# A transformer trunk on one core: the neighbourhood stage's keys and queries split once and arranged by DMA copies, its small softmax blocks scaled by a product with a broadcast

## The chip, the cores and the metric

One core of a Trainium2 chip. The metric is the device time of one execution in microseconds (us). The kernel before was executed three times: 2248.18, 2249.1 and 2251.29 us, median 2249.1 us.

## What is computed

Four residual steps in each of two layers, on 512 tokens of width 1024, all in float32: a half-step SwiGLU network, a token mixer, cross-attention into 256 memory tokens and a second half-step network, each followed by a layer norm. The mixer of the second layer is the one that the change touches, 2-D neighbourhood attention with 16 heads of width 64:

```python
def mixer_c(h, w_in, w_out, rpb):
    ...
    q, k, v = jnp.split(h @ w_in, 3, axis=-1)
    ...
    def row_block(r):
        rs = jnp.clip(r - kh // 2, 0, rows - kh)
        ...
        s = jnp.einsum('bwhd,bawjhd->bhwaj', q_r, k_nb).astype(jnp.float32) * scale
        s = s + bias.astype(jnp.float32)[None]
        p = jax.nn.softmax(s.reshape(B, C_HEADS, GRID_W, kh * kw), axis=-1)
        ...
        return jnp.einsum('bhwaj,bawjhd->bwhd', p, v_nb)
    ...
    return o @ w_out
```

## The kernel before

**Numbers.** A float32 operand is kept as two parts, high (rounded to the type that TensorE reads) and low (what is left), and each product is three matmuls (`mm3`, high x high, high x low, low x high). Making the two parts out of a PSUM bank takes a ScalarE instruction, which copies the high part, and a VectorE instruction, which subtracts it from the bank (`split`, line 293). Weights are loaded by SyncE (SP) into a `raw` tile of up to 1 MB and split in the same way (`weights`, line 310).

**Order.** No engine's order is written by hand. `Graph` records every operation (`record`, lines 128 to 163; every instruction is issued from the one call in it, so that the profile shows L140 throughout), and derives from overlapping tiles what must come before what. `emit` (lines 165 to 247) then plays the engines forward with a price for each operation (`cost`, line 110; a DMA of SP is priced at its bytes by 205 GB/s, at least 600 ns, and 2000 ns more until others may use it) and with the free buffers of each tag (`BUFS`: 14 of `t2`, 27 of `slab`, 2 of `raw`, and PSUM banks `a` 3, `d` 2, `t` 3), and issues the instructions engine by engine in the order that comes out. The semaphores are put in afterwards by the framework. All DMAs of SP share one hardware queue, and SP waits, in order, for what each of its DMAs needs.

**Stages.** ffn, mixer AB, memory, ffn, ffn, mixer C (`mixer_c`, line 914), memory, ffn. Mixer C goes by eight pairs of heads. For each pair `keys` (line 952) projects 128 columns into a `t` bank with 24 matmuls, and `queries` (line 937) into a `d` bank (the first pair's into `a` banks). The bank's rows 0 to 63 belong to the pair's first head, 64 to 127 to the second. The scores contract over 128 rows, of which a head fills 64; the other 64 hold further parts of the same head, so that two matmuls do for three: the queries' tile of a head has its high part on its own 64 rows and its low part on the other 64, and the keys have for each head one tile with the high part on both halves and one with the low part on both. Before, ScalarE and VectorE write these halves directly from the bank: per head one 64x512 instruction of each for the queries, and two of each for the keys.

`weights_of` (line 987) makes the scores of a head's four query blocks (`a` banks), adds the bias tables (`biases`, line 967, loaded by a DMA of POOL), and the softmax; blocks 0 and 3 (128x192) are scaled on VectorE, 1 and 2 (128x256) on POOL (`normalise`, line 618). `turned` (line 1017) transposes them into `t` banks and splits those; `attend` (line 1030) multiplies with the values into `d` banks. The main loop (line 1057) records, for a pair: keys of the next, `turned`, queries of the one after, `weights_of` the next, `attend`, and two blocks of `values`. The memory stages scale one 128x256 block in two on VectorE, in eight pairs per stage; `weights_a` in mixer AB scales blocks of 512 columns.

Of the kernel before, what the change touches and what calls it, by code (L numbers as in the profile page):

```python
# [12 lines left out]
F32 = mybir.dt.float32  # L13
# [3 lines left out]
AF = mybir.ActivationFunctionType  # L17
ALU = mybir.AluOpType
# [45 lines left out]
class Graph:  # L64
# [63 lines left out]
    def record(self, engine, method, args, kw):  # L128
        kw = dict(kw)
        aps = [z for z in list(args) + list(kw.values()) if hasattr(z, "tensor")]  # L130
        outs = [kw[k] for k in ("out", "accum_out") if k in kw]
        if "out" not in kw:
            outs.insert(0, args[0])
        ins = [z for z in aps if not any(z is o for o in outs)]
        op = Op()
        op.engine, op.index, op.dma = engine, len(self.ops), method == "dma_start"
        op.rank = op.index
        op.ns = self.cost(engine, method, outs[0], ins, kw)
        fn = getattr(getattr(self.nc, engine), method)
        op.call = lambda: fn(*args, **kw)  # L140
        op.deps, op.users, op.frees = set(), [], []
        if self.after and engine in self.after[1]:
            op.deps.add(self.after[0])
        for z, writes in [(z, False) for z in ins] + [(z, True) for z in outs]:
            info = self.tiles.get(z.tensor.name)
            if info is None:
                continue
            p0, p1, runs = self.extent(z)
            opens = writes and kw.get("start", False)
            keep = []  # L150
            for q, w, a0, a1, other in info["log"]:
                over = opens or p0 < a1 and a0 < p1 and (
                    info["bank"] and q.engine != engine or any(l < b and a < h for l, h in runs for a, b in other)
                )
                if over and (w or writes) and q is not op:
                    op.deps.add(q)
                covered = writes and p0 <= a0 and a1 <= p1 and all(any(l <= a and b <= h for l, h in runs) for a, b in other)
                if not covered:
                    keep.append((q, w, a0, a1, other))
            keep.append((op, writes, p0, p1, runs))  # L160
            info["log"] = keep
            info["users"].add(op)
        self.ops.append(op)
# [86 lines left out]
class Kernel:  # L250
# [365 lines left out]
        return h, l  # L616

    def normalise(self, u, r, on_vector):
        if on_vector:
            self.nc.vector.tensor_scalar(u, u, r, None, ALU.mult)  # L620
        else:
            self.nc.gpsimd.tensor_tensor(out=u, in0=u, in1=r.broadcast_to(list(u.shape)), op=ALU.mult)

    def softmax(self, u, rows, mn, lo, n, sums=None, on_vector=False):

# [288 lines left out]
    def mixer_c(self, ln_i, last):  # L914
        nc, a = self.nc, self.a
# [21 lines left out]
        def queries(pair, first=False):  # L937

            if pair % 2 == 0:
                wq[0] = self.w_cols(w_in, 128 * pair)  # L940
            ps = self.ps("a" if first else "d")
            for lo, hi in [(0, 128), (128, 256), (256, 512)] if first else [(0, 512)]:
                self.project(wq[0][pair % 2], ps, lo, hi)
            qs[pair] = self.pair()
            for s, z in enumerate(qs[pair]):
                own, other = slice(64 * s, 64 * s + 64), slice(64 - 64 * s, 128 - 64 * s)
                nc.scalar.activation(z[own], ps[own], AF.Copy, scale=-0.125)
                nc.vector.scalar_tensor_tensor(
                    out=z[other], in0=ps[own], scalar=-0.125, in1=z[own].bitcast(F32), op0=ALU.mult, op1=ALU.subtract
                )  # L950

        def keys(pair, first=False):

            if pair % 2 == 0:
                wk[0] = self.w_cols(w_in, D + 128 * pair)
            ps = self.ps("a" if first else "t")
            for lo, hi in [(0, 256), (256, 512)] if first else [(0, 512)]:
                self.project(wk[0][pair % 2], ps, lo, hi)
            ks[pair] = [self.pair() for _ in range(2)]
            for s, (h, l) in enumerate(ks[pair]):  # L960
                own, other = slice(64 * s, 64 * s + 64), slice(64 - 64 * s, 128 - 64 * s)
                for half in (own, other):
                    nc.scalar.copy(h[half], ps[own])
                for half in (own, other):
                    nc.vector.tensor_tensor(out=l[half], in0=ps[own], in1=h[own].bitcast(F32), op=ALU.subtract)

        def biases(pair):

# [88 lines left out]
        vp, qs, ks, acts = {}, {}, {}, []  # L1057
        wv, wq, wk, wo = [None], [None], [None], {}
        for t in range(NT):
            values(0, t)  # L1060
        queries(0, True)
        keys(0, True)
        queries(1)
        us = weights_of(0)
        for pair in range(8):


            if pair < 7:
                keys(pair + 1)
            else:  # L1070
                for n in range(3, 5):
                    share(n)
            pts = turned(us)
            if pair < 6:
                queries(pair + 2)
            else:
                for n in (0, 1) if pair == 6 else (5, 6, 7):
                    share(n)
            if pair < 7:
                us = weights_of(pair + 1)  # L1080
            acts.append(attend(pts, pair))
            if pair < 6:
                for t in range(2):
                    values(pair // 2 + 1, 2 * (pair % 2) + t)
            elif pair == 6:
                share(2)
# [200 lines left out]
```

## Time and profile before

| | |
|---|---|
| runs | 2248.18, 2249.1, 2251.29 us (median 2249.1) |
| profiled execution: its time | 2250.06 us |
| profiled execution: its span, first to last instruction | 2248.3 us |
| mean granted TensorE clock | 0.996 |
| stretch of mixer C | about 1495 to 1670 us |
| stretch of mixer AB | about 394 to 560 us |

PE is TensorE's matmuls, PEld its weight loads beside them, DVE is VectorE, ACT ScalarE, POOL GpSimd, SP SyncE. The span and the profiled execution's time differ by 1.8 us, which lie before the first and after the last instruction. `slab`, `t2` and `raw` are tiles in SBUF; `a`, `d` and `t` as an output of PE are PSUM banks, and since the views leave buffer numbers out, the `t2` tiles also appear there as `t`.

### The profile page before, as it was taken

How to read it: one execution, taken by the hardware profiler on the slowest of the kernel's cores; microseconds unless marked ns; L12 is line 12 of the kernel's file. 1: busy time of each engine (PE TensorE's matmuls, PEld its weight loads, DVE VectorE, ACT ScalarE, POOL GpSimd, SP SyncE). 2: the span in 40 equal slices, each digit the busy share in tenths (PEclk: the TensorE clock that was granted, in tenths of full speed). 3: DMA queues.
4: the chain of work that ended last, by engine and by line, in shares of the span. 5: the costliest groups of instructions: out<-in, count | busy, mean ns of one | idle time of the engine just before them, and what ended most of it. 6: DMA issues, size and time to landing. Idle time of an engine off the chain costs nothing. (4 is left out here: it accounts for less than half of the span.)

```text
span 2248.3 us, 28157 instructions
## 1 busy us (share of the span) xinstructions
PE 2207.0 (98%) x11312; PEld 1871.7 (83%) x11312; DVE 1420.1 (63%) x2116; ACT 882.7 (39%) x1418; POOL 287.0 (13%) x391
## 2 busy tenths in 40 slices
PE   8999999999999999999999999999999999999998
PEld 7888888778898888888888888888888988888886
DVE  5666646788745766665655667368776457666653
ACT  4323332566433433333333333256554434333331
POOL 0000203543000100001100003013411001000011
PEclk9999999999999999999999999999999999999999
DMA  6333241003333332225312334212233333322241
GB/s 207 129 120 113 67 154 57 20 20 90 124 106 113 113 113 90 72 83 168 105 40 86 113 117 150 75 62 68 69 113 96 129 113 113 113 82 72 85 137 38
DMA packets 168755, 221.09 MB, mean 98 GB/s; under 512 B 6192, under 2 KB 136880, under 8 KB 168624
## 3 DMA queue, kind: packets, MB, share of 16 engines
q1 hardware_dynamic: 165552, 208.80, 28.9%
q0 software_dynamic: 3072, 10.49, 1.3%
q8 instruction: 89, 1.46, 0.3%
q14 instruction: 42, 0.34, 0.1%
HBM read 217.17 MB, written 4.19 MB: 98 GB/s over the span
## 5 line engine op out<-in xcount | busy, mean ns | idle before, releaser
L140 PE MATMUL a<-xh,slab 128*128 128x512 f32 (+1 forms) x2960 | 890.8, 382 | 0.0
L140 PEld LDWEIGHTS a<-xh,slab 128*128 128x128 f32 x2960 | 549.1, 188 | 107.1
L140 PE MATMUL d<-slab,slab 128*128 128x512 f32 (+2 forms) x2432 | 572.5, 384 | 4.7 <-DVE slab L140 2.8
L140 PE MATMUL a<-xl,slab 128*128 128x512 f32 (+1 forms) x1480 | 565.0, 382 | 0.0
L140 PEld LDWEIGHTS d<-slab,slab 128*128 128x128 f32 x2432 | 441.1, 188 | 94.3 <-DVE slab L140 4.2
L140 ACT CAST slab<-raw 128x1024 fp32r<-128x1024 f32 x316 | 320.7, 1050 | 310.9 <-DMA raw<-ffn_w_gate 129.8
L140 DVE TENSOR_TENSOR slab<-raw,slab 128x1024 fp32r<-128x1024 f32 x316 | 391.6, 1254 | 72.9 <-ACT slab L140 55.4
L140 PEld LDWEIGHTS a<-xl,slab 128*128 128x128 f32 x1480 | 278.3, 188 | 53.0
L140 DVE TENSOR_TENSOR slab<-slab,slab 128x1024 fp32r<-128x1024 f32 (+2 forms) x208 | 241.4, 1184 | 18.9 <-ACT slab L140 17.6
L140 ACT CAST slab<-slab 128x1024 fp32r<-128x1024 f32 (+1 forms) x144 | 140.1, 1000 | 238.4 <-DVE slab L140 238.3
L140 ACT CAST slab<-t 128x512 fp32r<-128x512 f32 (+3 forms) x261 | 143.5, 572 | 225.9 <-DVE t L140 142.0
L140 PE MATMUL a<-slab,slab 128*128 128x256 f32 (+3 forms) x1336 | 204.9, 303 | 6.2 <-DVE slab L140 2.6
L140 DVE TENSOR_TENSOR slab<-a,t 128x512 f32<-128x512 f32 x56 | 38.7, 691 | 269.3 <-PE a L140 269.3
L140 PEld LDWEIGHTS a<-slab,slab 128*128 128x128 f32 x1336 | 180.6, 194 | 21.5 <-DVE slab L140 6.0
L140 DVE TENSOR_TENSOR slab<-t,slab 128x512 fp32r<-128x512 f32 (+3 forms) x261 | 164.3, 654 | 42.7 <-ACT slab L140 41.5
L140 DVE SCALAR_TENSOR_TENSOR x<-d,x 128x512 f32<-128x512 f32 x216 | 147.3, 685 | 48.3 <-PE d L140 47.3
L140 PE MATMUL t<-slab,slab 128*128 128x512 f32 (+1 forms) x648 | 152.1, 379 | 0.0
L140 ACT ACTIVATE t<-a 128x512 f32<-128x512 f32 (+2 forms) x104 | 57.4, 552 | 225.2 <-PE a L140 203.0
L140 POOL TENSOR_TENSOR x<-x,slab 128x512 f32<-128x512 f32 x24 | 46.0, 1950 | 780.7 <-DVE x L140 780.7
L140 PEld LDWEIGHTS t<-slab,slab 128*128 128x128 f32 x648 | 115.7, 188 | 25.0 <-DVE slab L140 2.2
L140 POOL TENSOR_TENSOR t<-t,l 128x256 f32<-128x256 f32 (+2 forms) x104 | 80.1, 785 | 308.4 <-DVE l L140 308.4
L140 PE MATMUL a<-slab,xh 128*128 128x256 f32 (+1 forms) x432 | 98.1, 319 | 4.1 <-ACT xh L140 4.0
(97 smaller groups left out, 1810.0 us busy)
## 6 DMA issues: line engine op xcount, KB each, us to landing
raw<-ffn_w_gate SPq DMA_DIRECT2D x40, 1024.0 KB
raw<-ffn_w_up SPq DMA_DIRECT2D x40, 1024.0 KB
slab<-ffn_w_down SPq DMA_DIRECT2D x64, 512.0 KB
raw<-ffn_w_down SPq DMA_DIRECT2D x12, 1024.0 KB
raw<-mem_w_kv SPq DMA_DIRECT2D x8, 1024.0 KB
raw<-mem_w_kv SPq DMA_DIRECT2D x16, 512.0 KB
raw<-mem_w_q SPq DMA_DIRECT2D x8, 1024.0 KB
raw<-mem_w_o SPq DMA_DIRECT2D x8, 1024.0 KB
```

Of the source, the lines that this page charges most:

```text
L140: op.call = lambda: fn(*args, **kw)
```

## The change

Three edits. In `record`, two reads of one PSUM bank by different engines become an ordering dependency of the planner. In `normalise`, blocks of up to 256 columns on VectorE are scaled with `tensor_tensor` and a broadcast of the reciprocal in place of `tensor_scalar`: 32 blocks of 128x192 in mixer C and 16 of 128x256 in the memory stages. In mixer C, each bank of keys or queries is split once, with all 128 rows, into two `t2` tiles, and SP copies halves of 64x512 (128 KB) from there into the same `slab` tiles as before: 4 copies per pair for the queries, 8 for the keys, 96 in all.

```diff
--- before.py
+++ after.py
@@ -152,7 +152,7 @@
                 over = opens or p0 < a1 and a0 < p1 and (
                     info["bank"] and q.engine != engine or any(l < b and a < h for l, h in runs for a, b in other)
                 )
-                if over and (w or writes) and q is not op:
+                if over and (w or writes or info["bank"] and q.engine != engine) and q is not op:
                     op.deps.add(q)
                 covered = writes and p0 <= a0 and a1 <= p1 and all(any(l <= a and b <= h for l, h in runs) for a, b in other)
                 if not covered:
@@ -616,10 +616,10 @@
         return h, l
 
     def normalise(self, u, r, on_vector):
-        if on_vector:
-            self.nc.vector.tensor_scalar(u, u, r, None, ALU.mult)
-        else:
-            self.nc.gpsimd.tensor_tensor(out=u, in0=u, in1=r.broadcast_to(list(u.shape)), op=ALU.mult)
+        if on_vector and u.shape[1] > 256:
+            return self.nc.vector.tensor_scalar(u, u, r, None, ALU.mult)
+        engine = self.nc.vector if on_vector else self.nc.gpsimd
+        engine.tensor_tensor(out=u, in0=u, in1=r.broadcast_to(list(u.shape)), op=ALU.mult)
 
     def softmax(self, u, rows, mn, lo, n, sums=None, on_vector=False):
 
@@ -941,13 +941,14 @@
             ps = self.ps("a" if first else "d")
             for lo, hi in [(0, 128), (128, 256), (256, 512)] if first else [(0, 512)]:
                 self.project(wq[0][pair % 2], ps, lo, hi)
+            parts = self.t2(), self.t2()
+            self.split(ps, *parts, scale=-0.125)
             qs[pair] = self.pair()
             for s, z in enumerate(qs[pair]):
-                own, other = slice(64 * s, 64 * s + 64), slice(64 - 64 * s, 128 - 64 * s)
-                nc.scalar.activation(z[own], ps[own], AF.Copy, scale=-0.125)
-                nc.vector.scalar_tensor_tensor(
-                    out=z[other], in0=ps[own], scalar=-0.125, in1=z[own].bitcast(F32), op0=ALU.mult, op1=ALU.subtract
-                )
+                for i, part in enumerate(parts):
+                    nc.sync.dma_start(
+                        out=z[64 * i : 64 * i + 64].bitcast(F32), in_=part[64 * s : 64 * s + 64].bitcast(F32)
+                    )
 
         def keys(pair, first=False):
 
@@ -956,13 +957,15 @@
             ps = self.ps("a" if first else "t")
             for lo, hi in [(0, 256), (256, 512)] if first else [(0, 512)]:
                 self.project(wk[0][pair % 2], ps, lo, hi)
+            parts = self.t2(), self.t2()
+            self.split(ps, *parts)
             ks[pair] = [self.pair() for _ in range(2)]
-            for s, (h, l) in enumerate(ks[pair]):
-                own, other = slice(64 * s, 64 * s + 64), slice(64 - 64 * s, 128 - 64 * s)
-                for half in (own, other):
-                    nc.scalar.copy(h[half], ps[own])
-                for half in (own, other):
-                    nc.vector.tensor_tensor(out=l[half], in0=ps[own], in1=h[own].bitcast(F32), op=ALU.subtract)
+            for s, both in enumerate(ks[pair]):
+                for z, part in zip(both, parts):
+                    for i in range(2):
+                        nc.sync.dma_start(
+                        out=z[64 * i : 64 * i + 64].bitcast(F32), in_=part[64 * s : 64 * s + 64].bitcast(F32)
+                    )
 
         def biases(pair):
```

The order on the engines around the keys of the fourth pair (pair 3), first **SP**. Before, only weight loads stand there (`raw_2340` is the keys' weights of pairs 4 and 5, `raw_2401` the queries' of 6 and 7, `raw_2331` and `raw_2438` are for values):

```order
L140 DMA raw_2294_2375<-c_w_in 128x8x256
L140 DMA raw_2331_2412<-c_w_in 128x4x256 x2
L140 DMA raw_2340_2421<-c_w_in 128x8x256
L140 DMA raw_2401_2482<-c_w_in 128x8x256
L140 DMA raw_2438_2519<-c_w_in 128x4x256 x2
L140 DMA raw_2447_2528<-c_w_in 128x8x256
```

After (`t2_2298` and `t2_2299` are the high and low part of the keys, `slab_2300` and `slab_2301` hold the keys' two tiles of the first and of the second head; `t2_2316` and `t2_2317` are the queries' parts of pair 4, and the first row is a copy of the queries of pair 3; `raw_2358` and `raw_2425` are the two loads named above):

```order
L140 DMA slab_2264_2345<-t2_2263_2344 64x512 x2
L140 DMA raw_2358_2439<-c_w_in 128x8x256
L140 DMA raw_2425_2506<-c_w_in 128x8x256
L140 DMA slab_2300_2381<-t2_2298_2379 64x512 x2
L140 DMA slab_2300_2381<-t2_2299_2380 64x512 x2
L140 DMA slab_2301_2382<-t2_2298_2379 64x512 x2
L140 DMA slab_2301_2382<-t2_2299_2380 64x512 x2
L140 DMA slab_2318_2399<-t2_2316_2397 64x512
L140 DMA slab_2318_2399<-t2_2317_2398 64x512
L140 DMA slab_2318_2399<-t2_2316_2397 64x512
```

Eight copies of the keys now stand in SP's queue, four for each head, and right ahead of them two weight loads of 1 MB; behind them are the four copies of the queries.

**ACT**, the same place. Before (`t_2283` is the keys' bank; the 128x512 casts split the transposes of the pair before):

```order
L140 CAST slab_2284_2365<-t_2283_2364 64x512 x2
L140 CAST slab_2285_2366<-t_2283_2364 64x512
L140 CAST slab_2287_2368<-t_2286_2367 128x512
L140 CAST slab_2289_2370<-t_2288_2369 128x512
L140 CAST slab_2285_2366<-t_2283_2364 64x512
L140 CAST slab_2291_2372<-t_2290_2371 128x512
L140 CAST slab_2293_2374<-t_2292_2373 128x512
L140 CAST slab_2341_2422<-raw_2340_2421 128x1024
L140 ACTIVATE slab_2300_2381<-d_2299_2380 64x512 x2
```

After (`t_2297` is the keys' bank):

```order
L140 CAST t2_2298_2379<-t_2297_2378 128x512
L140 CAST slab_2303_2384<-t_2302_2383 128x512
L140 CAST slab_2305_2386<-t_2304_2385 128x512
L140 CAST slab_2307_2388<-t_2306_2387 128x512
L140 CAST slab_2309_2390<-t_2308_2389 128x512
L140 CAST slab_2359_2440<-raw_2358_2439 128x1024
L140 ACTIVATE t2_2316_2397<-d_2315_2396 128x512
```

Four casts of 64 rows, with the splits of two transposed banks between them, have become one of 128 rows, ahead of all four transposed banks. The same holds on VectorE.

**PE**, after the keys of pair 3 and the first head's two transposes: `d_2299` is the bank of the queries of pair 4, the `ident` rows are the second head's transposes. Before, the last of the 14 matmuls into `d_2299` that stand ahead of those transposes, and what follows:

```order
L140 MATMUL d_2299_2380<-xh_2_83,slab_2295_2376 128x512
L140 MATMUL d_2299_2380<-xl_3_84,slab_2295_2376 128x512
L140 MATMUL t_2290_2371<-ident_1_78,t2_2266_2347 128x128 x3
L140 MATMUL t_2290_2371<-ident_1_78,t2_2267_2348 128x128
L140 MATMUL t_2292_2373<-ident_1_78,t2_2267_2348 128x128 x2
L140 MATMUL t_2292_2373<-ident_1_78,t2_2266_2347 128x128
L140 MATMUL t_2292_2373<-ident_1_78,t2_2267_2348 128x128
L140 MATMUL d_2299_2380<-xh_2_83,slab_2296_2377 128x512
```

After (the bank of queries is `d_2315`, and these are all of its matmuls that stand ahead):

```order
L140 MATMUL t_2304_2385<-ident_1_78,t2_2270_2351 128x128
L140 MATMUL d_2315_2396<-xh_2_83,slab_2311_2392 128x512
L140 MATMUL d_2315_2396<-xl_3_84,slab_2311_2392 128x512
L140 MATMUL d_2315_2396<-xh_2_83,slab_2312_2393 128x512
L140 MATMUL d_2315_2396<-xh_2_83,slab_2311_2392 128x512
L140 MATMUL t_2306_2387<-ident_1_78,t2_2280_2361 128x128 x3
L140 MATMUL t_2306_2387<-ident_1_78,t2_2281_2362 128x128
L140 MATMUL d_2315_2396<-xl_3_84,slab_2311_2392 128x512
L140 MATMUL t_2308_2389<-ident_1_78,t2_2281_2362 128x128 x2
L140 MATMUL t_2308_2389<-ident_1_78,t2_2280_2361 128x128
L140 MATMUL t_2308_2389<-ident_1_78,t2_2281_2362 128x128
```

The second head's transposes have moved forward, from behind 14 of the 24 query matmuls to behind 4.

## Rows read from the trace of the kernel before

**Rows 1.** The page's head: span, and busy time, share and instructions of engines.

```profile
span 2248.3 us, 28157 instructions
PE 2207.0 (98%) x11312; PEld 1871.7 (83%) x11312; DVE 1420.1 (63%) x2116; ACT 882.7 (39%) x1418; POOL 287.0 (13%) x391
```

**Rows 2.** Stretches (two ffn, mixer AB, mixer C): length, busy, clock, DMA.

```profile
1100.00:1475.00 375.00, 374.88 (x1793) 314.56 (x1792) 235.21 (x291) 127.34 (x166) 39.98 (x47) 1.00 0.29 96
394.00:560.00 166.00, 162.03 (x877) 134.18 (x876) 135.35 (x350) 103.51 (x248) 76.36 (x120) 1.00 0.16 40
1495.00:1670.00 175.00, 171.20 (x1046) 148.98 (x1045) 136.92 (x306) 112.72 (x257) 59.37 (x106) 1.00 0.23 76
```

**Rows 3.** Waits of PE in mixer C: us in total, times, longest.

```profile
PE t L140 <- DVE slab L140: 1.3, 3, 0.6
PE a L140 <- DVE mn L140: 1.2, 4, 0.6
PE d L140 <- DVE slab L140: 0.9, 4, 0.3
```

**Rows 4.** VectorE's groups in mixer C: count, busy, mean ns, idle before.

```profile
L140 DVE TENSOR_TENSOR slab<-t,slab 128x512 fp32r<-128x512 f32 x35 | 24.6, 734 | 0.4
L140 DVE TENSOR_TENSOR slab<-t,slab 64x512 fp32r<-64x512 f32 x28 | 19.3, 689 | 23.6 <-ACT slab L140 23.3
L140 DVE TENSOR_SCALAR t<-t,l 128x192 f32<-128x192 f32 x32 | 19.0, 632 | 0.3
...
L140 DVE CUSTOM_DVE_ANT_0 t<-a,t 128x192 f32<-128x192 f32 x32 | 10.8, 350 | 2.4 <-PE a L140 2.4
L140 DVE SCALAR_TENSOR_TENSOR slab<-d,slab 64x512 fp32r<-64x512 f32 x14 | 9.6, 689 | 1.3 <-ACT slab L140 1.1
```

**Rows 5.** ScalarE's groups in mixer C.

```profile
L140 ACT CAST slab<-t 128x512 fp32r<-128x512 f32 x35 | 19.8, 595 | 5.7 <-PE t L140 3.1 <-DVE t L140 2.3
L140 ACT CAST slab<-t 64x512 fp32r<-64x512 f32 x28 | 16.2, 580 | 30.8 <-PE t L140 25.3 <-DVE slab L140 5.2
...
L140 ACT ACTIVATE slab<-d 64x512 fp32r<-64x512 f32 x14 | 8.3, 593 | 10.0 <-PE d L140 9.9
```

**Rows 6.** Timeline around the keys of pair 3: start, us, engine, what.

```profile
1557.23 0.39 PE L140 MATMUL t<-xh,slab 128*128 128x512 f32 x1
...
1565.13 0.88 PE L140 MATMUL a<-slab,slab 128*128 128x192 f32 x6
1565.84 0.40 PE L140 MATMUL d<-slab,slab 128*128 128x256 f32 x2
...
1557.72 1.17 ACT L140 CAST slab<-t 64x512 fp32r<-64x512 f32 x2 [2.66 <-PE t L140]
...
1560.25 4.76 DVE L140 TENSOR_TENSOR slab<-t,slab 64x512 fp32r<-64x512 f32 x7 [0.65 <-ACT slab L140]
```

**Rows 7.** Timeline at the first pair: end of its keys, first scores.

```profile
1497.49 0.28 PE L140 MATMUL a<-xh,slab 128*128 128x256 f32 x1
...
1502.85 0.88 PE L140 MATMUL a<-slab,slab 128*128 128x192 f32 x6
```

**Rows 8.** DMAs of POOL (us to landing), and SP's issues (ns min/median/max).

```profile
t<-bias POOLq DMA_DIRECT2D x16, 128.0 KB, 2.4
...
L140 SPq DMA_DIRECT2D raw<-c_w_in x16: 367/368/529, 1404.1 to 1602.0; - x16
...
L140 SPq DMA_DIRECT2D bias<-rpb_g x16: 631/662/1044, 33.0 to 156.7; - x16
```

**Rows 9.** Timeline of one 1 MB load of SP and the cast that waits for it.

```profile
1176.86 0.37 SPq L140 DMA_DIRECT2D raw<-ffn_w_up  x1
...
1182.24 1.05 ACT L140 CAST slab<-raw 128x1024 fp32r<-128x1024 f32 x1 [2.90 <-DMA raw<-ffn_w_up]
```

**Rows 10.** Scaling on POOL in mixer C, on VectorE in the memory stages.

```profile
L140 POOL TENSOR_TENSOR t<-t,l 128x256 f32<-128x256 f32 x32 | 19.5, 627 | 33.2 <-DVE l L140 33.2
...
L140 DVE TENSOR_SCALAR t<-t,l 128x256 f32<-128x256 f32 x16 | 6.4, 400 | 0.2
```

## The prediction

> **What bounds the kernel now.** I read the page's head first: TensorE is busy for 2207.0 of the span's 2248.3 us, 98%, while VectorE stands at 63%, ScalarE at 39% and POOL at 13% [rows 1]. Then the stretches, since such a share is an average: in two ffn steps TensorE idles for 0.12 us of 375, in mixer AB for 166 − 162.03 = 3.97 us, in mixer C for 175 − 171.20 = 3.80 us, all at a granted clock of 1.00, the upper of its two levels, 2.4 GHz [rows 2]. The change issues the same matmuls, so it can only touch TensorE's idle time, and that of mixer C is the only one where it rewrites the work: 3.80 us there is nearly all there is to gain. The list of waits says what they are: 1.3 us for a `t` bank that VectorE still reads, 1.2 us for an `a` bank whose scores VectorE has not consumed, 0.9 us in front of `attend` for a split on VectorE [rows 3]. About 0.4 us is not named. One execution differs from the next by more than a tenth of a per cent; what a measurement can tell from no change here is about 0.2%, 4.5 us, more than mixer C's whole idle time.
>
> **Less work on ScalarE and VectorE.** Each pair's keys cost 4 halves of 64x512 on either engine and its queries 2; over eight pairs that is 48 on each, 42 of them in the groups (28 of keys, 14 of queries), the first pair's 6 are of the same kind. ScalarE: 32 × 0.580 + 16 × 0.593 = 28.1 us becomes 16 × 0.595 = 9.5 us, −18.6 us [rows 5]. VectorE: 48 × 0.689 = 33.1 us becomes 16 × 0.734 = 11.7 us, −21.3 us [rows 4]. Neither is on the path as busy time: TensorE is. What counts is when a bank comes free. The keys' bank of pair 3 is done at 1557.23 + 0.39 = 1557.62 us; ScalarE and VectorE then take turns on it, and VectorE's run on that bank and on the transposes ends at 1560.25 + 4.76 = 1565.01 us [rows 6]. Now the bank is read by one ScalarE and one VectorE instruction, 0.595 + 0.734, with the hand-over about 1.4 us. The second head's transposes, which wait for such a bank, stand behind 4 query matmuls in place of 14, which I cost at nothing, since the other 10 follow. I take the 1.3 us of the `t` waits as gone, and of the 1.2 and 0.9 us about half, 1.0 us, because VectorE, freed of 21 us, comes sooner to scores and splits. Gain 2.3 us; bounds 0 (the waits come from the order of one bank after another, and a new order brings new ones) and 3.8 us (all idle time of the stretch).
>
> **The copies.** The trace has no copy from SBUF to SBUF. What stands nearest is a 128 KB load of POOL, 2.4 us from issue to landing; SP's issue takes 0.37 us for weights and 0.66 us for the copies that build the bias tables [rows 8]. I take 0.37 us, because that is SP's price in this stage, and 0.66 as the upper bound. After the keys' end: 1.4 us for the split, then the first head's four copies, 4 × 0.37 = 1.5, and landing 2.4: 5.3 us. The second head's last copy is 4 × 0.37 later: 6.8 us. Needed: TensorE came to the first scores 1565.13 − 1557.62 = 7.5 us after the keys' end, with the same transposes and query matmuls between, in both orders. Its next six matmuls took 1565.84 − 1565.13 = 0.71 us, 0.12 each [rows 6]; the second head's scores come some 14 such matmuls later, 1.6 us: 9.1 us. So the slack is 2.2 us for either head, and a plain pair costs nothing. With 0.66 us per copy it is 1.4 + 2.6 + 2.4 = 6.4 and 1.4 + 5.3 + 2.4 = 9.1 us: just in time.
>
> Three places have less. At pairs 3 and 5 a weight load of 1 MB stands right ahead of the eight copies in the one queue (two stand there at pair 3). A load of 1 MB was 1182.24 − 1176.86 = 5.4 us from issue to its cast [rows 9], 3.0 us more than a 128 KB load, so I delay the copies by 3.0 us at most: 8.3 us against 7.5, 9.8 against 9.1. TensorE then stands for 0.8 us; 0.7 us each is my term, since the load is issued somewhat ahead of the copies, bounds 0 and 3.0 us. At the first pair the gap is short: keys end at 1497.49 + 0.28 = 1497.77 us, first scores at 1502.85, 5.1 us later [rows 7], against 5.3: 0.2 us, bounds 0 and 2.5 us (0.66 per copy, second head, 9.1 − 6.6). Sum of the copies +1.6 us, from 0 to 8.5.
>
> The queries' four copies per pair are needed a whole pair later, some 20 us, and hide behind the pair's matmuls. Weight loads queued behind copies wait until VectorE has split: at most the 1.4 us plus eight issues of 0.37, 4.4 us. Loads run a pair or more ahead, so I cost that at nothing; without that cover it would be 4.4 us at one pair. The four `t2` tiles per pair that are new may delay the bias tables on POOL by a load of 2.4 us; those are also made ahead of the scores: nothing.
>
> **The scaling.** On VectorE 32 blocks of 128x192 take 0.632 us each, although VectorE does a richer pass over the same columns, from a bank, in 0.350 us [rows 4]; beside them POOL scales its blocks at 0.627 us [rows 10], and in the memory stages, where 256 columns are scaled, it is 0.400 us. So the block is held up by POOL. A product with a broadcast lies between 0.35 us (the contact gone) and 0.63 + 0.35 = 0.98 us (it waits out a POOL instruction): 32 × (−0.28 to +0.35) = −9 to +11 us of VectorE. I take no change, as the nearest row is the same work at 0.63. It touches TensorE only by way of the waits priced above: nothing.
>
> **The planner's edit** forbids nothing that the chip did before; it shifts a few projections of mixer AB, whose 3.97 us of idle time [rows 2] bound the effect: 0, between −1 and +1 us.
>
> **Sum.** −2.3 + 1.6 = −0.7 us against the profiled 2250.06 us. That execution was 0.96 us above the median of 2249.1, so in terms of the median 2248.4 us. Bounds of this case: −3.8 − 1 and +8.5 − 2.3 + 1, so 2244.3 to 2256.3; as the copies' bounds hardly all come together, its own range is 2244.7 to 2253.5.
>
> **Rivals.**
> (1) Faster: the copies are hidden everywhere and the engines' relief removes all of mixer C's idle time and 1 us in mixer AB: 2249.1 − 4.8 = 2244.3 us. For it: VectorE and ScalarE end every one of those waits [rows 3]. Against it: it needs every wait gone.
> (2) Slower: SP's queue serves the copies one after another at 0.66 us or more. Its place is the score matmuls after the keys. It decides from 0.66 us per copy on plain pairs and from about 0.3 us where 1 MB stands ahead: (9.1 − 1.4 − 2.4 − 3.0) / 8. At 0.66 it costs 3.0 us at pairs 3 and 5 and 2.5 at the first: 8.5 − 2.3 = +6.2, 2255.3 us. For it: 12 DMAs per pair where there were two or three, in the queue that carries the weights. Against it: the queue's load is light, 0.23 of the DMA engines [rows 2]. The Trainium skill, page "SBUF — State Buffer", says under "Door 1: The DMA port swizzle (why [64,N] ≈ [32,N])" that 64 rows reach half of the DMA ports, about 218 GB/s, so that as an estimate 128 KB takes 0.6 us, and, under "Can I just issue two DMAs to hit both halves?", that transfers to the two halves serialise; by that rule this rival's price is about right, and the sum would be 2255 us. No run here shows it yet.
> (3) The scaling does what it is meant to and VectorE gains 9 us more: without effect on TensorE; within the forecast.
>
> **Chances.** Forecast (with 3) 0.50; rival 1 0.25; rival 2 0.25. Faster by over 0.2% (below 2244.6) is rival 1 at 0.22, with 0.03 of it falling short; slower (above 2253.6) rival 2 at 0.23; within 0.2% 0.55. The range of 8 in 10 reaches to both rivals: 2243 to 2256.5 us; the lower side ends 1.3 us under rival 1, since all idle time of mixer C is then gone, and the upper 1.2 us over rival 2.
>
> **What would show it.** Right: mixer C's idle time between 2 and 4.5 us; the list of waits without VectorE's `t` rows, and with a new wait of scores for `slab` from a DMA at the first pair and pairs 3 and 5, each under 1.5 us; no 64x512 splits of keys and queries, and two more of 128x512 per pair on either engine; the copies issued in about 0.37 us and landed in 2.4. Wrong: a wait for copies at plain pairs, a granted clock under 1.00 in mixer C, a scaling row near 0.35 or 0.98 us, or a change of the idle time in the ffn steps.

## The result, and the profile after

The changed kernel takes 2258.41 us (median of five runs, 2257.05 to 2260.46) against 2249.1 us: a ratio of 1.0039, 95% interval 1.0028 to 1.0050. It is 0.4% slower, 9.3 us, where 2248.4 us was forecast, and it lies 1.9 us above the upper end of the range. The profiled execution took 2258.08 us, with a span of 2256.3 us.

TensorE's work is the same, as expected: 11312 matmuls and the same busy time within 0.6 us, so in sum the 8 us of span are idle time, though single stages can differ in busy time too. First the head of the page after, against [rows 1]:

```profile
span 2256.3 us, 28354 instructions
PE 2206.4 (98%) x11312; PEld 1873.9 (83%) x11312; DVE 1395.8 (62%) x2084; ACT 863.3 (38%) x1386; POOL 286.1 (13%) x391
```

VectorE and ScalarE have lost 24.3 and 19.4 us of busy time, about the −21.3 and −18.6 us of the sum, and the kernel is slower. Where? Both programs issue the same number of matmuls in each stage, so one can ask of the n-th matmul how much later it starts than the n-th before. These differences are worked out from the starts in both traces (in us; the stage in which that matmul stands and its time before are beside it):

```
matmul no.   time before   behind by
   100          26           0.7     first loads
  1850         406           0.8     mixer AB, projections
  1925         422           4.4     mixer AB, first transposes and scores
  2000         438          10.5     mixer AB
  2300         495           9.9
  2850         599           8.8     memory
  7400        1497           8.4     mixer C begins
  7650        1542           6.5     mixer C, before the scores of pair 3
  7800        1566          10.0     mixer C, behind them
  8100        1614          11.5     mixer C, scores of pair 5
  8400        1664           8.8     mixer C ends
 11300        2235           8.0
```

The loss is not where the change rewrites the work. Mixer C as a whole costs 0.4 us; mixer AB, which only the planner's edit reaches, costs 8 to 10. In the same count of matmuls, from the 1850th to the 2600th, TensorE idles 5.4 us longer and is busy 3.5 us longer. The windows of the changed kernel, in the order of [rows 2] (the two ffn steps, mixer AB, mixer C):

```profile
1100.00:1475.00 375.00, 374.94 (x1771) 313.85 (x1770) 232.13 (x287) 126.57 (x164) 32.76 (x33) 1.00 0.29 96
394.00:560.00 166.00, 156.62 (x826) 128.51 (x826) 126.46 (x338) 97.41 (x238) 77.70 (x121) 0.98 0.13 33
1495.00:1670.00 175.00, 169.76 (x1076) 152.50 (x1076) 109.16 (x255) 87.09 (x209) 57.45 (x112) 0.99 0.53 140
```

Idle time in mixer AB has gone from 3.97 to 9.38 us, and the granted clock from 1.00 to 0.98. Smaller windows show when (same columns: busy times of TensorE, its weight loads, VectorE, ScalarE, POOL, then clock and DMA):

```profile
415.00:420.00 5.00, 2.56 (x13) 1.88 (x11) 1.68 (x9) 0.45 (x2) 3.83 (x6) 1.00 0.42 105
420.00:425.00 5.00, 4.91 (x19) 4.01 (x20) 2.96 (x12) 1.34 (x3) 2.40 (x5) 0.66 0.00 0
425.00:430.00 5.00, 4.85 (x23) 3.68 (x21) 3.82 (x6) 2.90 (x4) 0.74 (x1) 1.00 0.01 2
430.00:435.00 5.00, 4.20 (x20) 2.44 (x20) 4.34 (x13) 3.80 (x12) 3.04 (x3) 1.00 0.00 0
435.00:440.00 5.00, 2.56 (x9) 1.61 (x9) 3.68 (x12) 3.07 (x8) 4.14 (x5) 0.81 0.00 0
440.00:445.00 5.00, 5.00 (x23) 4.01 (x22) 2.31 (x4) 1.77 (x3) 0.32 (x1) 0.84 0.00 0
```

Two stalls, each in a window with 2.4 us of idle time, and with or behind each of them a lower mean clock: 0.66, then 0.81 and 0.84. The timeline of TensorE names the longest wait of each and shows the lower of the two levels (1.2 and 2.4 GHz) in the spacing of its matmuls of 512 columns, 0.43 us apart at 421 us where they are 0.23 apart at 416 us:

```profile
416.49 0.61 PE L140 MATMUL a<-slab,xh 128*128 128x512 f32 x2
416.95 0.39 PE L140 MATMUL a<-slab,xl 128*128 128x512 f32 x1
417.18 0.38 PE L140 MATMUL t<-ident,slab 128*128 128x128 f32 x2
420.09 1.09 PE L140 MATMUL t<-ident,slab 128*128 128x128 f32 x8 [2.53 <-POOL slab L140]
...
421.81 0.63 PE L140 MATMUL d<-slab,xl 128*128 128x512 f32 x1
422.24 1.05 PE L140 MATMUL d<-slab,xh 128*128 128x512 f32 x2
...
438.49 1.22 PE L140 MATMUL d<-slab,xh 128*128 128x512 f32 x2 [1.98 <-ACT t L140]
```

What is late there? In mixer AB a bank of the second half of the projections holds the A keys, the values and a part of the B queries, and both engines read it: ScalarE squares the keys (for their norm) and casts the values, VectorE subtracts for the values' low part, makes the products of the ropes (rotations by position) of the B queries, and multiplies the keys with their norm, which comes from POOL. VectorE's timeline in the changed kernel (start, us, what, and the wait before it):

```profile
412.72 0.28 DVE L140 TENSOR_TENSOR slab<-a,slab 128x128 fp32r<-128x128 f32 x1
412.92 0.81 DVE L140 TENSOR_TENSOR t<-a,slab 128x128 f32<-128x128 f32 x3
413.64 1.21 DVE L140 TENSOR_TENSOR slab<-raw,slab 128x1024 fp32r<-128x1024 f32 x1
414.78 0.28 DVE L140 TENSOR_REDUCE rh<-t 128x2 f32<-128x128 f32 x1
418.34 0.29 DVE L140 TENSOR_TENSOR t<-a,rms2y 128x128 f32<-128x128 f32 x1 [3.29 <-POOL rms2y L140]
418.67 0.56 DVE L140 TENSOR_TENSOR t<-t,slab 128x64 f32<-128x64 f32 x3
419.15 0.28 DVE L140 TENSOR_TENSOR slab<-a,slab 128x128 fp32r<-128x128 f32 x1
```

VectorE stands for 3.29 us between a block's sums (`rh`) and the multiply with the norm (`rms2y`), with the subtraction and the ropes' products on the same bank still to do (they follow at 419.15). For 1.84 us of that wait POOL zeroes the padded value tiles (from 415.40), which in the kernel before it did from 411.06, ahead of the norm's sums. In the kernel before, VectorE's instructions on the bank stood in that gap:

```profile
413.28 0.29 DVE L140 TENSOR_REDUCE rh<-t 128x2 f32<-128x128 f32 x1 [0.41 <-ACT t L140]
413.48 0.28 DVE L140 TENSOR_TENSOR t<-a,slab 128x128 f32<-128x128 f32 x1
413.68 0.28 DVE L140 TENSOR_TENSOR slab<-a,slab 128x128 fp32r<-128x128 f32 x1
413.88 0.42 DVE L140 TENSOR_TENSOR t<-a,slab 128x256 f32<-128x256 f32 x1
414.70 0.29 DVE L140 TENSOR_TENSOR t<-a,rms2y 128x128 f32<-128x128 f32 x1 [0.41 <-POOL rms2y L140]
```

In the kernel before, ScalarE reads a block twice in a row, square and then cast:

```profile
412.97 0.28 ACT L140 ACTIVATE t<-a 128x128 f32<-128x128 f32 x1 [4.26 <-POOL slab L140]
413.14 0.26 ACT L140 CAST slab<-a 128x128 fp32r<-128x128 f32 x1
```

After, it casts a block's values only when VectorE has multiplied, and squares the next block behind that cast, in its order:

```profile
412.24 0.27 ACT L140 CAST slab<-a 128x128 fp32r<-128x128 f32 x1 [5.41 <-DVE t L140]
412.40 0.28 ACT L140 ACTIVATE t<-a 128x128 f32<-128x128 f32 x1
418.67 0.27 ACT L140 CAST slab<-a 128x128 fp32r<-128x128 f32 x1 [5.99 <-DVE t L140]
418.83 0.28 ACT L140 ACTIVATE t<-a 128x128 f32<-128x128 f32 x1
```

So the blocks go one after another, each with its way to POOL and back. The last block's multiply, 418.71 us before, is at 422.07 us after. The edit in `record` was read in the forecast as something that the chip does anyway. A dependency also has a direction: it says that of two reads by different engines the one recorded first goes first. The code records square, multiply, cast, subtraction, ropes, and that became the order.

### The profile page after: what moved, and what is told of

Same layout as the page of the kernel before. It is cut to its first block, busy times and chain, and to the rows that moved or that the text cites. A ratio compares the mean times of both kernels' runs of the same rounds, so it can differ in the third digit from the quotient of the medians.

```text
span 2256.3 us, 28354 instructions
## 1 busy us (share of the span) xinstructions
PE 2206.4 (98%) x11312; PEld 1873.9 (83%) x11312; DVE 1395.8 (62%) x2084; ACT 863.3 (38%) x1386; POOL 286.1 (13%) x391
## 4 chain that ended last, share of the span: by engine, by line
PE 92%; DVE 3%; ACT 2%; DMA 1%; POOL 1%; issue 1%; SPq 0%; POOLq 0%; DVEq 0%; ACTq 0%
PE a L140 55%; PE d L140 25%; PE t L140 12%; DVE slab L140 1%; DVE x L140 1%; POOL lny L140 1%; DMA slab<-t 1%; ACT junk L140 0%; DMA x<-x 0%; ACT t L140 0%; DVE t L140 0%; ACT slab L140 0%; SPq L140 0%; DMA raw<-mem_w_kv 0%; ACT xh L140 0%
## 5 line engine op out<-in xcount | busy, mean ns | idle before, releaser
L140 ACT CAST slab<-t 128x512 fp32r<-128x512 f32 (+2 forms) x233 | 127.5, 570 | 209.6 <-DVE t L140 144.7
L140 DVE TENSOR_TENSOR slab<-t,slab 128x512 fp32r<-128x512 f32 (+2 forms) x233 | 145.3, 648 | 24.6 <-ACT slab L140 23.8
L140 ACT ACTIVATE t<-a 128x512 f32<-128x512 f32 (+3 forms) x105 | 58.1, 553 | 219.9 <-PE a L140 218.9
L140 POOL TENSOR_TENSOR t<-t,l 128x256 f32<-128x256 f32 (+2 forms) x104 | 85.1, 834 | 335.8 <-DVE l L140 321.1
```

## The experiments

All kernels are given against the kernel before, whose median lay between 2249.7 and 2250.1 us on these chips.

### One edit at a time

`e1_planner_only` is the kernel before with this line, the other three leave it out:

```diff
-                if over and (w or writes) and q is not op:
+                if over and (w or writes or info["bank"] and q.engine != engine) and q is not op:
```

> The kernel before with the planner's edit alone. Matmul for matmul, the changed kernel's trace ran 0.7 us behind at 400 us, 10.5 us behind at 450 us, in mixer AB, and 8.5 us behind when mixer C began, so the theory is that the planner's edit is the loss: 2249.1 + 7.7 = 2256.8 us (2255 to 2259), with the wait of transposes for POOL (2.5 us) and the one of a d bank for ScalarE (2.0 us) between 415 and 440 us. Rival, the copies are the loss (their DMAs, or the memory of the new tiles, also reach back to mixer AB): within 1 us of 2249.1.

Measured: 2255.65 us, ratio 1.0026 (1.0016 to 1.0036). 6.0 us slower by that one line, with both waits in TensorE's list for mixer AB (2.5 us for POOL, the longest of a `d` bank for ScalarE 2.0 us):

```profile
PE t L140 <- POOL slab L140: 2.9, 2, 2.5
PE d L140 <- ACT t L140: 2.6, 2, 2.0
```

The n-th matmul is 1.8 us behind at 406 us, 11.1 at 438, 10.2 when mixer C begins and 8.7 when it ends. So in this execution the edit gains 1.5 us in mixer C, and its full price stands in mixer AB.

`e2_copies_and_scaling` is the changed kernel without that line.

> The changed kernel without the planner's edit. Theory: mixer AB as before; mixer C gains about 2 us up to its third pair and gives it back at pairs 3 and 5, where scores wait for copies behind weight loads (2.7 and 1.2 us): 2249.1 + 0.3 - 0.8 at the memory stage = 2248.6 us (2247 to 2251). Rival, the copies are the loss: about 2257 us.

Measured: 2250.38 us, 1.0002 (0.9993 to 1.0011): no change that can be told. The rival, that the copies are the loss, falls. The parts, 6.0 us of this line and 0.7 of the rest, add up to 6.7 of the 9.3 us; the other 2.6 lie within the width of the intervals, and no run says more of them.

`e3_copies_only` is that without the edit of `normalise`.

> The kernel before with the copies alone. Theory: the scaling is off the path, so within 1 us of the kernel with copies and scaling, about 2248.6 us; the scaling's row of 128x192 back at 632 ns. Rival, the shorter scaling is what brought the 2 us in mixer C's first pairs: 2 us slower than that kernel, about 2250.6 us.

Measured: 2251.55 us, 1.0006 (0.9997 to 1.0015), 1.2 us above the run with the scaling; the intervals overlap, so neither is told from the other. Its runs spread from 2247.94 to 2253.35 us.

`e4_scaling_only` is the kernel before with the edit of `normalise` alone.

> The kernel before with the scaling alone; TensorE's order stays as it was. Theory: VectorE's 128x192 block goes from 632 to about 570 ns, 2 us of VectorE in all, and the time stays at 2249.1 us within 1 us. Rival, VectorE's earlier finish ends some of the 1.2 us of waits of score banks: 2248 us.

Measured: 2250.10 us, 1.0002 (0.9993 to 1.0011), no change. The row is at 606 ns, against 632 [rows 4]:

```profile
L140 DVE TENSOR_TENSOR t<-t,l 128x192 f32<-128x192 f32 x32 | 18.1, 606 | 0.3
```

### Which read comes first

In all of these the planner's edit is in. `e5_values_first` records the other readers of the bank ahead of the norm:

```diff
-            self.rope(self.rms(ps[:, 0:128], 2), 2, tabs["k"], t, ka[:, t])
             value(ps[:, 128:256], va, t)
             self.rope(ps[:, 256:512], 4, tabs["b"], t, pairs(qb[t], 0))
+            self.rope(self.rms(ps[:, 0:128], 2), 2, tabs["k"], t, ka[:, t])
```

> The changed kernel, with the values' split and the ropes of the B queries recorded ahead of the norm of the A keys, which reads the same bank in mixer AB. Theory: under the planner's edit each reader of such a bank waits for the reader recorded before it, so the split's cast on ScalarE waits for the norm's multiply, and with it, in ScalarE's order, the square of the next block: the last multiply came at 422.07 us in place of 418.71. With the cast recorded first that chain is gone: the 2.5 us wait of the transposes for POOL goes, and the low clock after it: 2258.4 - 4.5 = 2254 us (2252.5 to 2256). Rival, it is the number of ordered reads, not which comes first: no gain, 2257 to 2260 us.

Measured: 2259.03 us, 1.0038 (1.0026 to 1.0051). A miss: the time is the rival's. ScalarE's square, now recorded last, waits for VectorE's subtraction and ropes as the cast had waited for its multiply:

```profile
412.55 0.27 ACT L140 CAST slab<-a 128x128 fp32r<-128x128 f32 x1 [1.42 <-PE a L140]
417.70 0.28 ACT L140 ACTIVATE t<-a 128x128 f32<-128x128 f32 x1 [4.88 <-DVE t L140]
```

The cast is early and the square late: it had not been the cast alone. What both orders have in common is that the engines take turns on the bank: ScalarE, VectorE, ScalarE, VectorE.

`e6_copy_first` does the like for the `d` banks, whose readers are seven VectorE instructions and one ScalarE copy:

```diff
+                nc.scalar.copy(vt[:, t * P : (t + 1) * P], ps[:, 384:512])
                 self.rope(ps[:, 0:256], 4, tabs["b"], t, pairs(qb[t], 1))
                 self.rope(ps[:, 256:384], 2, tabs["b"], t, kb[:, t])
-                nc.scalar.copy(vt[:, t * P : (t + 1) * P], ps[:, 384:512])
```

> The changed kernel, with ScalarE's copy of the B values out of a d bank recorded ahead of the seven VectorE instructions that read that bank. Theory: the 2.0 us wait of TensorE for a d bank that ScalarE has not yet read goes, and the lower clock after it: 2258.4 - 3.5 = 2255 us (2253.5 to 2257). Rival, VectorE is late there anyway and the bank comes free no sooner: 2258.4 us.

Measured: 2257.34 us, 1.0033 (1.0020 to 1.0045). The wait for ScalarE's copy is gone from TensorE's list, but the lag at the 2000th matmul falls only from 10.5 to 8.2 us, and another 2.0 us are lost near 490 us. `e7_both_first` has both edits:

> The changed kernel with both recordings changed, and the planner's edit still in. Theory: mixer AB is as before within 2 us, 2258.4 - 8 = 2250.4 us (2248.5 to 2253). Rival, the planner's edit costs wherever it acts: 2254 us or more.

Measured: 2257.33 us, 1.0031 (1.0019 to 1.0043). The time is the rival's, but not its reason: `f2_scalar_reads_first` below has the planner's edit in and loses next to nothing.

`e8_memset_vector` takes from POOL the zeroing that stood on the chain:

```diff
-            self.nc.gpsimd.memset(z.bitcast(F32), 0.0)
+            self.nc.vector.memset(z.bitcast(F32), 0.0)
```

> The changed kernel with the zeroing of the padded value tiles on VectorE in place of POOL. In the changed kernel 1.84 us of it stand on POOL between the sums of the third A-key block (ready at 415.06 us) and their square root (417.33 us), on the chain for which the transposes waited 2.5 us. Theory: 1.8 us of that wait go, and a part of the low clock: 2258.4 - 2.5 = 2256 us. Rival, ScalarE's order alone sets that wait and POOL has room: no change, 2258.4 us.

Measured: 2259.88 us, 1.0041 (1.0028 to 1.0053). It now stands in VectorE's order ahead of the same block's sums, and the wait of the transposes grew from 2.5 to 4.0 us:

```profile
416.29 0.91 DVE L140 MEMSET slab<- 128x1024 f32 x1 [0.16 <-issue]
417.37 0.91 DVE L140 MEMSET slab<- 128x1024 f32 x1 [0.16 <-issue]
418.20 0.23 DVE L140 TENSOR_REDUCE rh<-t 128x2 f32<-128x128 f32 x1
```

`f1_square_and_cast_first` acts on the turns: both of ScalarE's reads of the bank are recorded in a row, then all of VectorE's. (`rms` takes a function that it calls behind its square, and `value` can do its cast and its subtraction apart.)

```diff
-            self.rope(self.rms(ps[:, 0:128], 2), 2, tabs["k"], t, ka[:, t])
-            value(ps[:, 128:256], va, t)
+            k = self.rms(ps[:, 0:128], 2, lambda: value(ps[:, 128:256], va, t, part=0))
+            self.rope(k, 2, tabs["k"], t, ka[:, t])
+            value(ps[:, 128:256], va, t, part=1)
```

> The changed kernel, with ScalarE's two reads of the A-key banks of mixer AB (the square and the values' cast) recorded one after the other, ahead of all of VectorE's. Theory: the loss comes from the two engines taking turns on one bank: square, multiply, cast, then subtraction and ropes, each waiting for the other engine, with the 3 us way to POOL and back in between; in the kernel before VectorE's ropes filled that time. With both ScalarE reads first they fill it again, and the first of the two stalls (3.6 us between 417 and 425 us) goes: 2258.4 - 3.6 = 2254.8 us (2253 to 2256.5). Rival, the chain over POOL is too long however it is ordered, as recording the values first left it: 2258 us or more.

Measured: 2252.97 us, 1.0014 (1.0005 to 1.0023): 5.4 us less than the changed kernel, more than forecast, and the intervals are apart. The lag at the 1925th matmul is 0.8 us in place of 4.4, and at the 2000th 5.2 in place of 10.5. ScalarE's square and cast again stand in a row, as in the kernel before.

`f2_scalar_reads_first` adds the edit of `e6_copy_first`.

> As the run before, and ScalarE's copy out of the d banks first as well. Theory: both stalls go (3.6 and about 4.9 us), less what a new order loses near 490 us (2.0 us in the run with that copy alone): 2258.4 - 6.5 = 2252 us (2250 to 2254). Rival, as above: 2257 us, as in the run with both first in the other way.

Measured: 2250.97 us, 1.0004 (0.9995 to 1.0013), with the planner's edit in. At 438 us, where the changed kernel is 10.5 us behind, this one is 0.8. VectorE again fills the time in which POOL makes the norm, and waits 0.92 us for it in place of 3.29:

```profile
413.73 0.27 DVE L140 TENSOR_REDUCE rh<-t 128x2 f32<-128x128 f32 x1
413.93 0.28 DVE L140 TENSOR_TENSOR slab<-a,slab 128x128 fp32r<-128x128 f32 x1
414.12 0.81 DVE L140 TENSOR_TENSOR t<-a,slab 128x128 f32<-128x128 f32 x3
415.86 0.29 DVE L140 TENSOR_TENSOR t<-a,rms2y 128x128 f32<-128x128 f32 x1 [0.92 <-POOL rms2y L140]
```

`f3_scalar_reads_first_no_planner_edit` is the same without the planner's edit.

> The run before without the planner's edit. Theory: without the ordering of reads it matters little which read is recorded first: within 1.5 us of copies and scaling alone, 2250.4 us. Rival, the recording itself is better or worse than the old one: over 2 us from it.

Measured: 2249.24 us, 1.0001 (0.9992 to 1.0010). Without ordered reads the recording hardly matters, as the theory has it. It is 1.7 us under the run with the planner's edit, and the intervals overlap.

### The copies at pairs 3 and 5

Mixer C's own list of waits after, against [rows 3]:

```profile
PE a L140 <- DMA slab<-t: 3.8, 4, 1.9
PE a L140 <- DVE mn L140: 2.4, 5, 1.0
```

The `t` and `d` waits are gone, and scores now wait for copies, at pair 3 (1.89 and 0.79 us) and pair 5 (0.98 and 0.19 us) alone. In SP's timeline at pair 3 two weight loads stand ahead of the copies, the second 2.6 us behind the first, since it waits for a free tile:

```profile
1561.91 3.01 SPq L140 DMA_DIRECT2D raw<-c_w_in  x2
1565.01 6.53 SPq L140 DMA_DIRECT2D slab<-t  x8
```

SP's order did not hold up the issue: ScalarE's cast of the keys ends at 1564.98 us and the first copy is issued at 1565.01. What was late was the data. The windows of the changed kernel at pair 2, with no load near, and at pair 3 (columns as above; the last two are the DMA engines' share and GB/s):

```profile
1543.00:1547.00 4.00, 4.00 (x23) 3.39 (x22) 2.30 (x4) 1.22 (x3) 0.59 (x1) 1.00 0.85 208
1565.00:1569.00 4.00, 4.00 (x25) 3.36 (x23) 3.38 (x6) 3.08 (x5) 1.11 (x2) 1.00 1.07 342
```

In those 4 us at pair 3 the DMA engines are full, and in the trace's packets 1.37 MB of the loads moved and nothing of a copy.

`f4_keys_copies_on_pool` issues the keys' copies from POOL, out of that order (`nc.sync.dma_start` becomes `nc.gpsimd.dma_start` in `keys`), in the kernel of `e2_copies_and_scaling`.

> Copies and scaling without the planner's edit, with the keys' copies issued by POOL instead of SP. Theory: at pairs 3 and 5 the copies are late because they stand behind two weight loads in SP's order, one of which waits 2.2 us for a free tile; on POOL they don't, and the waits of scores for a DMA (3.7 us) go: 2250.4 - 3.5 = 2247 us. Rival 1, the weights occupy the DMA engines whoever issues: the waits stay, 2250.4 us. Rival 2, eight issues of 0.55 us per pair on POOL hold up its scaling of two blocks in four: 2253 us or more.

Measured: 2260.04 us, 1.0045 (1.0032 to 1.0057): rival 2. POOL's issues take 33.2 us, and TensorE's waits for scores to be consumed by VectorE grow to 6.6 us; a wait of 2.8 us for a copy at the first pair is new. No scores wait for a copy at pairs 3 and 5, but as TensorE comes later to every pair, this says little of the weight loads.

`g1_loads_behind_copies` holds those loads instead, in the kernel of `f3_scalar_reads_first_no_planner_edit`: before the keys' loads (and the queries' load for pair 6, and the first of `c_w_out`) POOL copies one column out of the keys tile that was copied last into the tile to be loaded.

```diff
         raw = self.tile(self.raw, [P, *shape], F32, "raw")
+        if self.hold is not None:
+            nc.gpsimd.tensor_copy(raw[:, 0, 0:1], self.hold[:, 0:1].bitcast(F32))
+            self.hold = None
```

> Copies and scaling with ScalarE's reads first, without the planner's edit, and with the weight loads that stood ahead of the copies of pairs 3 and 5 held until these have landed (one column of the load's tile is first written by POOL from the copied keys). Theory: the copies were late because of those loads: the waits of scores for a DMA (3 to 4 us) go at both pairs, and mixer C ends some 5 us ahead of the kernel before: 2249.2 - 3.5 = 2245.7 us (2244 to 2247.5), 0.2% under the kernel before. Rival, eight copies issued one after another are late there by themselves: no change, 2249.2 us. Second rival, the held loads come late for the next pair's projections: 2252 us or more.

Measured: 2250.82 us, 1.0003 (0.9994 to 1.0012). The waits for a DMA at pairs 3 and 5 are gone, so the loads ahead were their cause: behind pair 3, at the 7900th matmul, this kernel is 2.3 us ahead of the kernel before. By the 8000th it is 0.7 behind. Two other waits for a DMA have come (0.23 and 1.07 us), though no load was moving there (the DMA engines' share is 0.00 at 1537 to 1538 us and 0.04 at 1630 to 1632, just before those copies), and the waits for VectorE grew from 2.4 to 4.7 us; the cause of these stays open. TensorE's timeline, the longest of the waits that are left and the first of the two for a copy:

```profile
1542.58 0.33 PE L140 MATMUL a<-slab,slab 128*128 128x192 f32 x1 [0.23 <-DMA slab<-t]
...
1595.17 0.47 PE L140 MATMUL a<-slab,slab 128*128 128x192 f32 x2 [1.47 <-DVE mn L140]
...
1636.47 0.62 PE L140 MATMUL a<-slab,slab 128*128 128x192 f32 x3 [1.07 <-DMA slab<-t]
...
1664.89 0.47 PE L140 MATMUL a<-slab,slab 128*128 128x192 f32 x2 [1.05 <-DVE mn L140]
```

`g2_loads_behind_copies_planner` is the same with the planner's edit.

> The run before with the planner's edit in, so the changed kernel with its reads and loads reordered. Theory: with ScalarE's reads first the edit costs 1 to 2 us at most: 2246 to 2248 us. Rival, it is still the loss of mixer AB: 2250 us or more.

Measured: 2250.53 us, 1.0002 (0.9993 to 1.0011). With the reads and loads reordered no price of the edit can be told; the forecast gain does not come. No version here is told from the kernel before on the faster side.

## Why the prediction was wrong, step by step

**The step that failed: the planner's edit "forbids nothing that the chip did before ... 0, between −1 and +1 us".** Alone it costs 6.0 us. Two errors lie in it. The idle time of a stretch (3.97 us) bounds what an edit can gain there, and not what it can lose. And the edit was judged by whether two reads can overlap, when what it does is fix which of them goes first. (That two such reads do not overlap holds where the trace can tell: none of ScalarE's 64x512 reads of the keys' banks overlapped one of VectorE's in the kernel before.) The new order of VectorE on those banks stood in the program before any run, and the forecast looked at the orders of mixer C alone. Idle time grew by 9.38 − 3.97 = 5.4 us in that stretch; the other 3.5 us came as slower matmuls, most of them where the granted clock was lower.

**ScalarE and VectorE relieved, −18.6 and −21.3 us, off the path.** Right in size (−19.4 and −24.3 us over the span), and off the path: the run with copies and scaling alone shows no change.

**Gain of 2.3 us in mixer C.** Near in size, in part by luck. Between the begin of mixer C and pair 3 the changed kernel makes up 1.9 us, and the `t` and `d` waits of [rows 3] are gone. The `a` waits are not: 2.4 us after 1.2. And of the 1.9 us only 0.8 are idle time. The other 1.2 are busy time, which the forecast held fixed ("it can only touch TensorE's idle time"): over the 1000 matmuls of mixer C, from the 7400th, the same work takes 2.1 us less, most of it in the transposes, which take 94 ns each from start to start in place of 111. Why is not shown.

**Copies, +1.6 us.** The places were right, pairs 3 and 5, with nothing on plain pairs and nothing at the first; the size was not: 2.7 and 1.2 us of waits, 3.9 in all, and 3.5 us of lag at pair 3. The 0.7 us for each pair rested on a load "issued somewhat ahead of the copies"; the nearest was issued 0.46 us ahead of the first copy at pair 3 and 0.47 at pair 5. The issue of a copy was taken at 0.37 us, from SP's row for weights; it is 0.59 us, near the upper bound of 0.66:

```profile
L140 SPq DMA_DIRECT2D slab<-t x96: 461/588/1239, 1501.1 to 1666.1; - x96
```

So rival 2's pace is what came, and its price came only where a load stands ahead, as its second threshold had it. The Trainium skill's rule on 64 rows ("SBUF — State Buffer", "Door 1: The DMA port swizzle (why [64,N] ≈ [32,N])"), about 218 GB/s, would as an estimate give 0.6 us for 128 KB, about the same pace. In the trace the copies moved at 246 GB/s from 1572 to 1575 us, a little above that figure, with the DMA engines full; at pair 2 the engines were 0.85 busy, which speaks for SP's issues as what sets the pace there, but no run changes one without the other. Mixer C as a whole came out at +0.4 us against −0.7.

**Scaling, no change.** Right for the time. The 128x192 block takes 567 ns after, inside the bounds of 0.35 to 0.98 us; the 128x256 block of the memory stages, 400 ns [rows 10], takes 489 ns as a product, 1.4 us more for these 16, off the path. That POOL held up the block before, as the forecast concluded, was not tested.

**Rivals and chances.** The slower side was right, with 0.23, by another mechanism than rival 2, so by luck. The upper bound of 2256.3 us was also added up wrongly: it took the gain at −2.3 us, though that term's own bound was 0, and with 0 it is 2249.1 + 8.5 + 1 = 2258.6 us. That would have held the measured time, but by late copies and not by the planner's edit. Of the signs of being wrong one came: the granted clock in mixer C is 0.99. Its idle time is 5.24 us, outside the 2 to 4.5 that were to show the forecast right.

## What to carry to other kernels

A dependency added to a planner costs by its direction, even where the two accesses did not overlap before: before pricing one at nothing, compare the order of each engine that shares the resource, in every stage that it reaches, not only where the change is meant to act. Where a planner keeps the reads of one bank in the order of recording, try recording all reads of the one engine and then all of the other; here ScalarE's first gave back 7.4 of the 9.3 us, and other orders gave back 1.1 us or nothing. And idle time in a stretch is a ceiling on a gain only.

## What the runs showed of the hardware

In the changed kernel the clock fell behind both stalls. From 420 to 425 us, with a wait of 2.53 us that ends at 420.09, TensorE was granted 0.66 of full speed, though it was busy for 4.91 of the 5 us; around a wait of 1.98 us it was 0.81 and 0.84. That is up to (1 − 0.66) × 5 = 1.7 us and (0.19 + 0.16) × 5 = 1.8 us, on top of the waits. With the stalls removed (the run with ScalarE's reads first) the same stretch has 1.00. But not every such wait has that price: with the planner's edit alone a wait of 2.54 us, and with the copy first one of 2.52 us, ended near 421 us, and the granted clock from 420 to 425 us was 1.00 in both. No run tells what decides it. A copy of 128 KB from SBUF to SBUF costs SP 0.59 us to issue, against 0.37 us for a weight load of 1 MB. Copies issued 0.46 us behind a load of 1 MB moved no data for the next 4 us, while the loads kept the DMA engines full at 342 GB/s.
